# Seeding the accumulation bank with the running sum, one tile ahead, and moving five modulation tiles from the attention into the input projection

## The chip, the cores and the metric

The kernel runs on one core of one Trainium2 chip. The metric is the device time of one execution in microseconds (us); the kernel before takes 2125.85 us, the median of three runs (2124.03 to 2126.39). In what follows PE is TensorE (the matmuls), DVE is VectorE, ACT is ScalarE, POOL is GpSimd, and SP is the engine that issues most of the DMAs.

## The reference

It is one layer of a diffusion backbone: 512 latent tokens of width 2048, with 256 context tokens as a prefix that the attention reads. Cut to what matters:

```python
mod_l = (silu(c) @ w_ada + b_ada);  mod_c = (silu(c_ctx) @ w_ada + b_ada)
sh_a, sc_a, gt_a, sh_f, sc_f, gt_f = split(mod_l, 6)
h_l = modulate(rms_norm(x, g_mix_norm), sh_a, sc_a)        # h * (1 + scale) + shift
h_c = modulate(rms_norm(ctx, g_mix_norm), csh_a, csc_a)
qa, kva, kr, cb, cc, ch = split_projection(h_l @ w_in)     # 512, 256, 64, 3 x 1024 columns
k, v = mla_key_value(kva, kr, g_kv_a, w_kv_b, rope)        # the same for h_c
q = mla_query(qa, g_q_a, w_q_b, rope)
att = block_attention(q, [k_l, k_c], [v_l, v_c])           # 8 heads, softmax in f32
conv = cb * dwconv3(cc * ch, conv_w, conv_b)
x = x + gt_a * (rms_norm_per_group([att, conv]) @ w_out)
u = dwconv3(modulate(rms_norm(x), sh_f, sc_f) @ w_up);  a, g = split(u, 2)
x = x + gt_f * ((a * silu(g)) @ w_down)
return rms_norm(x, g_final)
```

The modulation vectors are products of one vector with the 2048 x 12288 matrix w_ada. The input projection has 3904 columns; transposed, these are 31 tiles of 128 columns by 512 tokens. The sum over the 2048 input features is 16 blocks of 128, called k-tiles below.

## The kernel before, in words

All large products keep float32 accuracy by splitting each operand into a high and a low part; every product is then three matmuls (mm3, lines 202 to 204). The split of a weight block is a cast on ACT for the high part (line 181) and a subtraction on DVE for the low part (line 182), from a raw buffer that a DMA has filled (line 150). There are two raw buffers for the weights of the projection.

The stages, by the trace: start until 24 us; input projection until about 396; preparation of queries, keys and values until about 447; attention in 32 steps until about 622; output projection until about 805; the gated MLP's up projection until about 1660; its down projection until the end.

The **input projection** goes through the 16 k-tiles in three chunks (ci = 0, 1, 2 with 2, 4 and 10 k-tiles), so that work can begin before all of the normalised input is there. Each chunk makes a partial sum for all 31 output tiles in PSUM. In chunks 1 and 2 the first six tiles (called pf) are computed together as rows; the other 25 (called pp) follow one after the other. In chunk 0 the partial sum of a tile is copied to a tile acc in SBUF by ACT. In chunks 1 and 2 the function evac adds the partial sum to acc on DVE (line 678):

```python
V.tensor_tensor(out=acc[m], in0=acc[m], in1=ps, op=ALU.add)
```

PSUM has eight banks. Four are handed out singly, four in two tiles of two banks each; two output tiles that share such a pair also share its waits, so that the first matmul into the second half waits for the read-out of the first half.

Beside this, **ctx_mods** (line 667) computes the context's 32 modulation columns with 64 products on DVE, called dots here. Each takes a half of a modulation tile (128 x 1024) that SP loads into one of four buffers; a new load must wait until a dot has freed its buffer. One or two dots are let loose per projection tile. Further modulation tiles, called **late**, are needed only after the attention. late_both lets one be loaded and an earlier one be multiplied; the loop of chunk 2 calls it at tiles i = 20 to 22 (two loads), and the attention's loop loads the rest at its steps n (late_load, line 1150 and those around it).

The order of the work on each engine is that of a scheduler that simulates the engines' timeline, except where keep(...) fixes program order. So a change in the program's text can also move instructions that it doesn't touch. The other two functions of the change are gn_sum (sums of squares per group, four one-column matmuls into one bank) and ctx_stats (the context's normalisation, spread over the partitions by a matmul into the bank rcb).

Of the kernel before, what the change touches and what calls it, by code (L numbers as in the profile page):

```python
# [11 lines left out]
F32R = mybir.dt.float32r  # L12
AF = mybir.ActivationFunctionType
ALU = mybir.AluOpType
# [17 lines left out]
G = 6  # L32
# [43 lines left out]
def block_kernel(ctx, tc, xt, ctxt, ctxn, c, c_ctx, w_ada, small, w_in, w_inc, w_q, w_kv, w_out,  # L76
# [313 lines left out]
    def gn_sum(t, o):  # L390
        sq = tmp([P, T], F32, f"gq{t}")
        A.activation(sq, o, AF.Square)
        yield
        ps = sml(f"gp{t}")
        for g in range(4):
            PE.matmul(ps[:, g:g + 1], sq[:, g * P:(g + 1) * P], ones[:, 0:1], start=True, stop=True)
        V.tensor_copy(out=gn[:, 4 * t:4 * t + 4], in_=ps[:, :4])
        yield

# [29 lines left out]
    with ExitStack() as pa:  # L429
# [197 lines left out]
        def ctx_stats():  # L627
            ss = tiny(4, "ss")
            for i in range(2):
                for q, r in enumerate(ada_tiles(p_sb, 4, ctxn[i], f"cn{i}")):  # L630
                    A.activation(r, r, AF.Square, accum_out=ss[:, 2 * i + q:2 * i + q + 1])
                    yield
            r = tiny(2, "rsc")
            V.tensor_tensor(out=r, in0=ss[:, 0:4:2], in1=ss[:, 1:4:2], op=ALU.add)
            rsqrt(r, r, D)
            yield
            pb = sml("rcb")
            spread(pb, r)
            A.copy(out=rc, in_=pb[:, :C])
            yield  # L640

        def ctx_prep(g):
# [27 lines left out]
        cm = ctx_mods()  # L670
        acc = {}

        def evac(ci, m, ps):
            if ci == 0:
                acc[m] = t2([P, T], F32, f"acc{m}")
                A.copy(out=acc[m], in_=ps)
                return
            V.tensor_tensor(out=acc[m], in0=acc[m], in1=ps, op=ALU.add)  # L678
            if ci < 2:
                return  # L680
            if m == 3:
                bg.appendleft(low_rank([acc[i] for i in range(4)], "g_q", T, "qa", qan))
            elif m == 5:
                bg.appendleft(low_rank([acc[i] for i in (4, 5)], "g_kv", T, "kl", kvl))
            elif m == 6:
                bg.appendleft(rope_key())
            elif m >= 9 and m % 3 == 0:
                q = bg if m < 27 else post
                q.append(conv((m - 9) // 3))
                q.append(gn_sum((m - 9) // 3, acc[m]))  # L690
                late_bg.append(gn_apply((m - 9) // 3, acc[m]))
# [137 lines left out]
        for ci, k0, n in ((1, K0[1], KCH[1]), (2, K0[2], KCH[2])):  # L829
# [21 lines left out]
            if ci == 1:  # L851
                ordered[0] = False
            per, step = max(1, 2048 // (n * P)), max(1, 4 // n)
            for i, m in enumerate(ORDER[G:]):
                if i % per == 0:
                    k = min(per, len(ORDER) - G - i) * n
                    raw = load(w_in[:, off:off + k * P], k * P, f"rw{ci}_{m}", G_ if ci == 1 else None)
# [1 line left out]
                if i % step == 0:  # L859
                    ws = blocks(raw, min(step, len(ORDER) - G - i) * n, f"w{ci}_{m}", i % per * n)  # L860
                w = ws[i % step * n:(i % step + 1) * n]
                ps = bank(f"pp{ci}_{m}")
                for kk in range(n):
                    mm3(ps, w[kk], hl[k0 + kk], kk == 0, kk == n - 1)
                evac(ci, m, ps)
                for f, j in todo.get((ci, i), []):
                    f(j)
                if ci == 2:
                    for q in range(2 if i % 4 == 0 else 1):
                        next(cm, None)  # L870
                    if 20 <= i <= 22:
                        late_both((lambda t: ada_tiles(p_sb, 4, w_ada[t], f"ae{t}")) if i < 22 else None)
                    if i >= 5 and i % 2 == 1 and (i - 5) // 2 < CTX_EARLY:
                        bg.append(ctx_prep((i - 5) // 2))
                    pump(2)
# [30 lines left out]
    with ExitStack() as pb:  # L906
# [215 lines left out]
        for n, st in enumerate(steps):  # L1122
# [23 lines left out]
                f(p_, i)  # L1146
            if at < 2 and n < 24:
                fetch(pr + 1, 2 + at)
            elif (at >= 2 or n == 24) and n <= 24:
                late_load(ada_raw)  # L1150
                if at == 6 and n < 16:
                    fetch(pr + 2, 0)
            if n == 8:
# [819 lines left out]
```

## Time and profile before

| | |
|---|---|
| median of three runs | 2125.85 us (2124.03 to 2126.39) |
| profiled execution | 2129.29 us |
| its span, first to last instruction | 2127.5 us |
| mean granted TensorE clock | 0.994 of full speed |
| PE busy | 2088.2 us (98%) |
| DVE busy | 1821.0 us (86%) |
| ACT busy | 1049.5 us (49%) |
| DMA | 514.78 MB, 242 GB/s on average |

A row of the profile names line, engine, operation, the tile written and the tiles read (buffer numbers left out), and the shapes. A bracket at its end gives the time that the engine stood idle before it and what released it. The granted clock is the share of full speed at which TensorE was allowed to run.

### The profile page before, as it was taken

Reading aid. Unit: us, or ns where it says so; the run is one execution under the profiler, and the core shown is the slowest. Engines: PE = TensorE matmul, PEld = TensorE weight load, DVE = VectorE, ACT = ScalarE, POOL = GpSimd, SP = SyncE. Lnnn points to the kernel's source line nnn. Section 1 sums busy time; section 2 is a strip of 40 time slices with the busy share of each in tenths; the row PEclk is TensorE's granted clock in tenths of the full one; section 3 lists DMA queues with packets and bytes.
Section 4 is the critical chain, followed back from the end, with each engine's and each line's share of the span. In section 5 each row is a group of like instructions: output and inputs, shape, how many; then the busy total and the mean of one; then the engine's idle time right before and its main releaser. Section 6 shows DMA issues by size and latency. Waiting matters only on the chain.

```text
span 2127.5 us, 35260 instructions
## 1 busy us (share of the span) xinstructions
PE 2088.2 (98%) x13303; PEld 1880.9 (88%) x13303; DVE 1821.0 (86%) x2952; ACT 1049.5 (49%) x1715; POOL 127.7 (6%) x161
## 2 busy tenths in 40 slices
PE   8999999999999999999999999999999999999997
PEld 6777778889888889999999999999999889999997
DVE  7898987878887888898999999999999659887887
ACT  6534233555552337555555655655555333333445
POOL 0000000000010000111000000000000000000000
PEclk9999999999999999999999999999999999999999
DMA  9799877435658975577888878888888989878684
GB/s 343 278 323 325 298 263 236 138 129 198 208 191 325 335 284 164 154 223 212 226 232 238 235 220 239 240 228 230 240 229 231 366 304 309 246 230 240 195 237 136
DMA packets 165885, 514.78 MB, mean 242 GB/s; under 512 B 18641, under 2 KB 22993, under 8 KB 155985
## 3 DMA queue, kind: packets, MB, share of 16 engines
q1 hardware_dynamic: 127024, 407.90, 56.7%
q0 software_dynamic: 19312, 70.40, 15.7%
q10 hardware_dynamic: 19378, 34.23, 4.2%
q8 instruction: 104, 1.70, 0.3%
q14 instruction: 67, 0.55, 0.1%
HBM read 465.26 MB, written 46.14 MB: 240 GB/s over the span
## 4 chain that ended last, share of the span: by engine, by line
PE 88%; DVE 5%; DMA 3%; issue 2%; ACT 2%; POOL 0%; DVEq 0%; SPq 0%; ACTq 0%; POOLq 0%
PE pp L202 3%; PE pp L204 3%; PE pp L203 3%; PE o L202 1%; PE o L204 1%; PE o L203 1%; PE d L202 1%; PE d L203 1%; PE d L204 1%; PE uf L202 1%; PE uf L203 1%; PE uf L204 1%; PE of L202 1%; PE of L204 1%; PE of L203 1%
## 5 line engine op out<-in xcount | busy, mean ns | idle before, releaser
L1445 POOL DMA_DIRECT2D u_s<-in_w_up x80 | 68.4, 855 | 682.5 <-DMA u_s<-in_w_up 402.9
L285 DVE SCALAR_TENSOR_TENSOR ada<-ada,sv 128x2048 f32<-128x2048 f32 x33 | 75.5, 2289 | 16.0 <-DMA ada<-in_w_ada 15.6
L181 ACT CAST w_0h<-rw 128x512 fp32r<-128x512 f32 x50 | 30.5, 620 | 99.2 <-DMA rw<-in_w_in 49.8
L667 DVE SCALAR_TENSOR_TENSOR ada<-ada,svc 128x1024 f32<-128x1024 f32 x64 | 76.1, 1217 | 1.9 <-DMA ada<-in_w_ada 1.9
L1566 DVE TENSOR_TENSOR u<-u,u_s 128x1024 f32<-128x1024 f32 x40 | 48.7, 1218 | 4.0 <-DMA u_s<-in_w_up 4.0
L281 DVE SCALAR_TENSOR_TENSOR ra<-ra,sv 128x1024 f32<-128x1024 f32 x42 | 49.8, 1216 | 0.0
L256 DVE SCALAR_TENSOR_TENSOR ada<-ada,sv 128x1024 f32<-128x1024 f32 x40 | 48.3, 1213 | 0.8 <-DMA ada<-in_w_ada 0.8
L1567 DVE TENSOR_TENSOR u<-u,u 128x1024 f32<-128x1024 f32 x40 | 48.6, 1216 | 0.0
L182 DVE TENSOR_TENSOR w_0l<-rw,w_0h 128x512 fp32r<-128x512 f32 x50 | 33.9, 682 | 15.4 <-ACT w_0h L181 15.2
L1071 POOL TENSOR_TENSOR gr<-gr,half 128x8 f32<-128x8 f32 x4 | 11.2, 2809 | 488.1 <-DVE gr L1070 458.1
L1365 DVE TENSOR_TENSOR tp<-a,tp 128x256 fp32r<-128x256 f32 x90 | 37.5, 416 | 2.9 <-ACT tp L1364 2.9
L1364 ACT CAST tp<-a 128x256 fp32r<-128x256 f32 x90 | 35.7, 403 | 6.6 <-DMA yl6h<-y_d 3.7
L1042 ACT CAST pth<-t 128x384 fp32r<-128x384 f32 x64 | 28.6, 486 | 18.0 <-PE t L1039 17.9
L1043 DVE TENSOR_TENSOR ptl<-t,pth 128x384 fp32r<-128x384 f32 x64 | 33.1, 548 | 3.9 <-ACT pth L1042 3.9
L1328 ACT ACTIVATE g<-g 128x512 f32<-128x512 f32 x43 | 27.2, 634 | 18.0 <-DVE g L1322 17.7
L678 DVE TENSOR_TENSOR acc<-acc,pp 128x512 f32<-128x512 f32 x50 | 33.8, 677 | 1.5 <-PE pp L204 1.5
L1021 DVE TENSOR_REDUCE mn<-s 128x1 f32<-128x768 f32 x32 | 30.3, 950 | 4.9 <-PE s L1010 4.9
L1320 ACT ACTIVATE g<-cg,sm 128x512 f32<-128x512 f32 x40 | 32.6, 815 | 0.0
L1320 ACT ACTIVATE a<-ca,sm 128x512 f32<-128x512 f32 x40 | 32.1, 802 | 0.0
L1024 ACT ACTIVATE p<-s,mn 128x768 f32<-128x768 f32 x32 | 29.3, 914 | 4.3 <-DVE mn L1021 4.1
L1321 DVE SCALAR_TENSOR_TENSOR g<-cg,sm,g 128x511 f32<-128x511 f32 x40 | 29.8, 745 | 0.0
L1321 DVE SCALAR_TENSOR_TENSOR a<-ca,sm,a 128x511 f32<-128x511 f32 x40 | 29.8, 745 | 0.0
(10435 smaller groups left out, 8966.4 us busy)
## 6 DMA issues: line engine op xcount, KB each, us to landing
ada<-in_w_ada SPq DMA_DIRECT2D x128, 512.0 KB, 5.9
u<-in_w_up SPq DMA_DIRECT2D x120, 512.0 KB, 9.2
w<-t_d SPq DMA_DIRECT2D x161, 256.0 KB, 5.3
u_s<-in_w_up SPq DMA_DIRECT2D x80, 512.0 KB, 4.0
u_s<-in_w_up POOLq DMA_DIRECT2D x80, 512.0 KB, 9.7
ada<-in_w_ada SPq DMA_DIRECT2D x33, 1024.0 KB, 6.2
t_d<-tp ACTq DMA_DIRECT2D x126, 256.0 KB, 6.0
v<-in_w_dnw SPq DMA_DIRECT2D x72, 384.0 KB, 5.7
```

The source lines that it names most:

```text
L202: PE.matmul(ps, w[0], x[0], start=first, stop=False, skip_group_check=on_top)
L203: PE.matmul(ps, w[0], x[1], start=False, stop=False, skip_group_check=on_top)
L204: PE.matmul(ps, w[1], x[0], start=False, stop=last, skip_group_check=on_top)
L256: ins = V.scalar_tensor_tensor(out=r, in0=r, scalar=1.0, in1=vec[:, i * 1024:(i + 1) * 1024], op0=ALU.mult, op1=ALU.mult, accum_out=col[:, ...
L281: keep(V.scalar_tensor_tensor(out=halves[i], in0=halves[i], scalar=1.0, in1=svs[i], op0=ALU.mult, op1=ALU.mult, accum_out=lc[:, t % 4:t % ...
L285: keep(V.scalar_tensor_tensor(out=r, in0=r, scalar=1.0, in1=sv, op0=ALU.mult, op1=ALU.mult, accum_out=mod[:, t:t + 1]))
L667: keep(V.scalar_tensor_tensor(out=raw[q], in0=raw[q], scalar=1.0, in1=svc[:, q * 1024:(q + 1) * 1024], op0=ALU.mult, op1=ALU.mult, accum_o ...
L1320: A.activation(u, src, AF.Identity, bias=s("fb", m), scale=s("fw", 86 + m))
L1321: V.scalar_tensor_tensor(out=u[:, 1:], in0=src[:, :T - 1], scalar=s("fw", m), in1=u[:, 1:], op0=ALU.mult, op1=ALU.add)
L1445: G_.dma_start(r[-1], src[more], accum_op=ALU.add)
L1566: V.tensor_tensor(out=a11, in0=a11, in1=s1, op=ALU.add)
L1567: V.tensor_tensor(out=a12, in0=a12, in1=a11, op=ALU.add)
```

## The change

Three things are different in the text.

1. In chunks 1 and 2, for the 25 pp tiles each: ACT copies acc into the PSUM bank of the **next** tile (seeded, line 864 of the changed kernel), before the current tile is multiplied. The matmuls then all add to what is in the bank (start=False), and ACT copies the finished sum back to acc (line 683). The addition on DVE stays for the six pf tiles of each chunk (line 685).
2. In gn_sum DVE writes zeros into the bank's four columns first, and its matmuls add to them; in ctx_stats a matmul with a zero operand is put behind the copy out of the bank rcb.
3. The loop of chunk 2 calls late_both at i = 17 to 24 in place of 20 to 22, with seven loads in place of two; the attention's loop has no late loads at steps 20 to 24 any more.

```diff
--- before.py
+++ after.py
@@ -392,8 +392,9 @@
         A.activation(sq, o, AF.Square)
         yield
         ps = sml(f"gp{t}")
+        V.tensor_scalar(ps[:, :4], ones[:, :4], scalar1=0.0, scalar2=None, op0=ALU.mult)
         for g in range(4):
-            PE.matmul(ps[:, g:g + 1], sq[:, g * P:(g + 1) * P], ones[:, 0:1], start=True, stop=True)
+            PE.matmul(ps[:, g:g + 1], sq[:, g * P:(g + 1) * P], ones[:, 0:1], start=False, stop=True, skip_group_check=True)
         V.tensor_copy(out=gn[:, 4 * t:4 * t + 4], in_=ps[:, :4])
         yield
 
@@ -637,6 +638,9 @@
             pb = sml("rcb")
             spread(pb, r)
             A.copy(out=rc, in_=pb[:, :C])
+            none = tmp([P, T], F32R, "none")[:, :P]
+            V.tensor_scalar(none, ones, scalar1=0.0, scalar2=None, op0=ALU.mult)
+            PE.matmul(pb, none, hl[K0[2]][0], start=False, stop=True, skip_group_check=True)
             yield
 
         def ctx_prep(g):
@@ -670,12 +674,15 @@
         cm = ctx_mods()
         acc = {}
 
-        def evac(ci, m, ps):
+        def evac(ci, m, ps, whole_sum=False):
             if ci == 0:
                 acc[m] = t2([P, T], F32, f"acc{m}")
                 A.copy(out=acc[m], in_=ps)
                 return
-            V.tensor_tensor(out=acc[m], in0=acc[m], in1=ps, op=ALU.add)
+            if whole_sum:
+                A.copy(out=acc[m], in_=ps)
+            else:
+                V.tensor_tensor(out=acc[m], in0=acc[m], in1=ps, op=ALU.add)
             if ci < 2:
                 return
             if m == 3:
@@ -851,7 +858,15 @@
             if ci == 1:
                 ordered[0] = False
             per, step = max(1, 2048 // (n * P)), max(1, 4 // n)
+
+            def seeded(m):
+                ps = bank(f"pp{ci}_{m}")
+                A.copy(out=ps, in_=acc[m])
+                return ps
+
+            nxt_ps = seeded(ORDER[G])
             for i, m in enumerate(ORDER[G:]):
+                ps, nxt_ps = nxt_ps, seeded(ORDER[G + i + 1]) if G + i + 1 < len(ORDER) else None
                 if i % per == 0:
                     k = min(per, len(ORDER) - G - i) * n
                     raw = load(w_in[:, off:off + k * P], k * P, f"rw{ci}_{m}", G_ if ci == 1 else None)
@@ -859,17 +874,16 @@
                 if i % step == 0:
                     ws = blocks(raw, min(step, len(ORDER) - G - i) * n, f"w{ci}_{m}", i % per * n)
                 w = ws[i % step * n:(i % step + 1) * n]
-                ps = bank(f"pp{ci}_{m}")
                 for kk in range(n):
-                    mm3(ps, w[kk], hl[k0 + kk], kk == 0, kk == n - 1)
-                evac(ci, m, ps)
+                    mm3(ps, w[kk], hl[k0 + kk], False, kk == n - 1, on_top=True)
+                evac(ci, m, ps, True)
                 for f, j in todo.get((ci, i), []):
                     f(j)
                 if ci == 2:
                     for q in range(2 if i % 4 == 0 else 1):
                         next(cm, None)
-                    if 20 <= i <= 22:
-                        late_both((lambda t: ada_tiles(p_sb, 4, w_ada[t], f"ae{t}")) if i < 22 else None)
+                    if 17 <= i <= 24:
+                        late_both((lambda t: ada_tiles(p_sb, 4, w_ada[t], f"ae{t}")) if i < 24 else None)
                     if i >= 5 and i % 2 == 1 and (i - 5) // 2 < CTX_EARLY:
                         bg.append(ctx_prep((i - 5) // 2))
                     pump(2)
@@ -1146,8 +1160,9 @@
                 f(p_, i)
             if at < 2 and n < 24:
                 fetch(pr + 1, 2 + at)
-            elif (at >= 2 or n == 24) and n <= 24:
-                late_load(ada_raw)
+            elif at >= 2 and n < 24:
+                if n < 20:
+                    late_load(ada_raw)
                 if at == 6 and n < 16:
                     fetch(pr + 2, 0)
             if n == 8:
```

How this moves instructions at three places:

The first place is the start of chunk 2's pp tiles, tiles 13 and 14, which share a pair of banks. On DVE before, with the pf additions of chunk 2 (pf20 to pf24), dots of ctx_mods (ada180, ada181) and the addition of tile 13 (acc13):

```order
L678 TENSOR_TENSOR acc8_403<-acc8_403,pf21_1555 128x512
L678 TENSOR_TENSOR acc9_405<-acc9_405,pf22_1556 128x512
L182 TENSOR_TENSOR w2_14_0l_1975<-rw2_14_1972,w2_14_0h_1974 128x512
L307 SCALAR_TENSOR_TENSOR scc0_2553<-modc_91,sm_82 128x2
L678 TENSOR_TENSOR acc10_407<-acc10_407,pf23_1557 128x512
L667 SCALAR_TENSOR_TENSOR ada181_1712,lcc_281<-ada181_1712,svc_99 128x1024
L678 TENSOR_TENSOR acc11_431<-acc11_431,pf24_1558 128x512
L678 TENSOR_TENSOR acc12_433<-acc12_433,pf24_1558 128x512
L604 TENSOR_TENSOR acc7_401<-acc7_401,acc8_403 128x512
L678 TENSOR_TENSOR acc13_435<-acc13_435,pp2_13_1924 128x512
L182 TENSOR_TENSOR w2_15_0l_2029<-rw2_15_2026,w2_15_0h_2028 128x512
```

On ACT in the changed kernel, at the same place, with the seeds of tiles 15 to 18, the casts of the weights of tiles 14 and 15, and the copy of tile 13's sum:

```order
L864 COPY pp2_15_2002<-acc15_468 128x512
L181 CAST w2_14_4h_2010<-rw2_14_2004 128x512
L864 COPY pp2_16_2058<-acc16_470 128x512
L608 ACTIVATE acc8_403<-acc7_401,sm_82 128x512
L640 COPY rc_280<-rcb_1783 128x256
L181 CAST w2_14_8h_2014<-rw2_14_2004 128x256
L864 COPY pp2_17_2119<-acc17_500 128x512
L864 COPY pp2_17_2119<-acc18_502 128x512
L181 CAST w2_15_0h_2062<-rw2_15_2060 128x512
L181 CAST w2_15_4h_2066<-rw2_15_2060 128x512
L683 COPY acc13_435<-pp2_13_1938 128x512
```

The read-out of tile 13 has gone from DVE, where it stood behind the pf additions, to ACT, where it stands behind two casts of tile 15's weights and four seeds.

The second place is SP's queue around the weights of tiles 20 to 22 of chunk 2 (rw2_20 to rw2_22), with halves of modulation tiles (ada) between them. Before:

```order
L150 DMA rw2_20_2317<-in_w_in 128x1280
L150 DMA ada231_2133<-in_w_ada 128x1024
L150 DMA ada70_2187<-in_w_ada 128x1024
L150 DMA ada71_2189<-in_w_ada 128x1024
L150 DMA ada240_2193<-in_w_ada 128x1024
L150 DMA ada241_2195<-in_w_ada 128x1024
L150 DMA ada80_2252<-in_w_ada 128x1024
L150 DMA ada81_2254<-in_w_ada 128x1024
L150 DMA rw2_21_2376<-in_w_in 128x1280
L150 DMA ada250_2308<-in_w_ada 128x1024
L150 DMA ada251_2310<-in_w_ada 128x1024
L150 DMA rw2_22_2438<-in_w_in 128x1280
```

Now:

```order
L150 DMA rw2_20_2358<-in_w_in 128x1280
L150 DMA ada231_2168<-in_w_ada 128x1024
L150 DMA ada70_2222<-in_w_ada 128x1024
L150 DMA ada71_2224<-in_w_ada 128x1024
L150 DMA ada240_2228<-in_w_ada 128x1024
L150 DMA rw2_21_2418<-in_w_in 128x1280
L150 DMA ada241_2230<-in_w_ada 128x1024
L150 DMA ada80_2290<-in_w_ada 128x1024
L150 DMA ada81_2292<-in_w_ada 128x1024
L150 DMA rw2_22_2481<-in_w_in 128x1280
L150 DMA ada250_2347<-in_w_ada 128x1024
L150 DMA ada251_2349<-in_w_ada 128x1024
```

The seven halves between the weights of tiles 20 and 21 have become four.

The third place is DVE near the end of the attention: the softmax maxima of successive steps (mn), the dots of the last late tiles (ra53, ra54), the splits of the output projection's first weights (ofw0) and the scaling of two output tiles (o4, o5). Before:

```order
L281 SCALAR_TENSOR_TENSOR ra54_5702,lc_94<-ra54_5702,sv_93 128x1024
L403 SCALAR_TENSOR_TENSOR acc21_559<-acc21_559,sm_82,gb4_5735 128x512
L1021 TENSOR_REDUCE mn70_5807<-s70_5761 128x1
...
L281 SCALAR_TENSOR_TENSOR ra53_5629,lc_94<-ra53_5629,sv_93 128x1024
...
L1021 TENSOR_REDUCE mn71_5842<-s71_5823 128x1
L182 TENSOR_TENSOR ofw0_0l_6042<-ofr0_5924,ofw0_0h_6041 128x512
L182 TENSOR_TENSOR ofw0_4l_6046<-ofr0_5924,ofw0_4h_6045 128x512
...
L182 TENSOR_TENSOR ofw0_8l_6050<-ofr0_5924,ofw0_8h_6049 128x512
L1081 SCALAR_TENSOR_TENSOR o4_5261<-o4_5261,sm_82,gb4_5793 128x512
L1081 SCALAR_TENSOR_TENSOR o5_5537<-o5_5537,sm_82,gb5_5799 128x512
```

Now:

```order
L281 SCALAR_TENSOR_TENSOR ra53_5416,mod_90<-ra53_5416,sv_93 128x1024
L281 SCALAR_TENSOR_TENSOR ra53_5416,lc_94<-ra53_5416,sv_93 128x1024
...
L281 SCALAR_TENSOR_TENSOR ra54_5470,mod_90<-ra54_5470,sv_93 128x1024
L281 SCALAR_TENSOR_TENSOR ra54_5470,lc_94<-ra54_5470,sv_93 128x1024
L182 TENSOR_TENSOR ofw0_0l_6113<-ofr0_5995,ofw0_0h_6112 128x512
L182 TENSOR_TENSOR ofw0_4l_6117<-ofr0_5995,ofw0_4h_6116 128x512
...
L1035 TENSOR_REDUCE mn53_5594<-s53_5564 128x1
L182 TENSOR_TENSOR ofw0_8l_6121<-ofr0_5995,ofw0_8h_6120 128x512
...
L1035 TENSOR_REDUCE mn60_5664<-s60_5612 128x1
```

Relative to the softmax steps, the last dots and the splits of ofw0 come five to seven steps earlier.

## Prediction

> **What bounds the kernel now.** I read the page's busy times and chain first, then the windows by stage, and after that the timelines of the stages that the change touches. The page says that the program is a row of matmuls:
>
> ```profile
> PE 2088.2 (98%) x13303; PEld 1880.9 (88%) x13303; DVE 1821.0 (86%) x2952; ACT 1049.5 (49%) x1715; POOL 127.7 (6%) x161
> ...
> PE 88%; DVE 5%; DMA 3%; issue 2%; ACT 2%; POOL 0%; DVEq 0%; SPq 0%; ACTq 0%; POOLq 0%
> ```
>
> TensorE is busy for 2088.2 of 2127.5 us. Nothing in the change takes matmuls away, so all that it can win is time in which TensorE stands still, plus time in which it runs at a lowered clock. The windows (columns: length, then busy time of PE, PEld, DVE, ACT, POOL, granted clock, DMA share, GB/s) tell in which stage that is:
>
> ```profile
> 88.00:158.00 70.00, 69.53 (x300) 56.07 (x299) 70.00 (x135) 26.65 (x40) 2.65 (x5) 1.00 0.87 307
> 158.00:316.00 158.00, 147.51 (x630) 118.58 (x629) 137.96 (x272) 52.93 (x96) 0.00 (x0) 0.96 0.86 297
> 316.00:360.00 44.00, 44.00 (x190) 35.40 (x189) 34.75 (x67) 13.19 (x24) 0.00 (x0) 1.00 0.83 280
> 344.00:412.00 68.00, 67.37 (x304) 54.12 (x302) 51.87 (x99) 29.32 (x58) 0.00 (x0) 1.00 0.47 157
> ```
>
> The second chunk of the projection (88 to 158) keeps TensorE full, although VectorE is full as well. From 316 on TensorE is full again, at 44.00/190 = 0.232 us a matmul. Only 158 to 316, the third chunk's first half, loses 10.5 us of busy time and has a clock of 0.96. The timeline of TensorE there names the stalls (idle time and releaser in brackets):
>
> ```profile
> 214.26 0.79 PE L202 MATMUL pp<-h6h,w_0h 128*128 128x512 f32 x1 [4.25 <-DVE acc L678]
> 247.33 0.51 PE L202 MATMUL pp<-h6h,w_0h 128*128 128x512 f32 x1 [1.41 <-ACT w_0h L181]
> 248.35 0.50 PE L204 MATMUL pp<-h6h,w_0l 128*128 128x512 f32 x1 [0.28 <-DVE w_0l L182]
> 280.28 0.50 PE L202 MATMUL pp<-h6h,w_0h 128*128 128x512 f32 x1 [2.48 <-ACT w_0h L181]
> 281.95 0.80 PE L204 MATMUL pp<-h6h,w_0l 128*128 128x512 f32 x1 [0.85 <-DVE w_0l L182]
> ```
>
> They are 4.25 + 1.69 + 3.33 = 9.27 us. After the first and the last the clock drops, in windows laid on its steps:
>
> ```profile
> 212.49:219.32 6.83, 5.06 (x12) 4.00 (x13) 6.83 (x12) 0.81 (x1) 0.00 (x0) 0.50 0.71 243
> 246.63:253.46 6.83, 5.85 (x24) 4.46 (x25) 6.83 (x14) 1.77 (x3) 0.00 (x0) 1.00 0.93 306
> 280.76:287.59 6.83, 5.98 (x15) 4.46 (x14) 6.83 (x12) 2.69 (x7) 0.00 (x0) 0.50 0.87 267
> ```
>
> At clock 0.50 work of 5.06 us would have taken half, so the first drop costs 2.53 us and the other 5.98/2 = 2.99 us; behind the 1.41 us wait the clock stays at 1.00. The stage's recoverable time is 9.27 + 2.53 + 2.99 = 14.8 us.
>
> [...]
>
> **Why these stalls are there.** The 4.25 us stall waits for the addition of acc13 on VectorE (L678). What VectorE does ahead of it:
>
> ```profile
> 206.30 0.69 DVE L678 TENSOR_TENSOR acc<-acc,pf 128x512 f32<-128x512 f32 x1 [0.98 <-PE pf L204]
> ...
> 206.97 1.22 DVE L667 SCALAR_TENSOR_TENSOR ada<-ada,svc 128x1024 f32<-128x1024 f32 x1
> ...
> 208.12 1.28 DVE L678 TENSOR_TENSOR acc<-acc,pf 128x512 f32<-128x512 f32 x2
> ...
> 210.59 1.22 DVE L667 SCALAR_TENSOR_TENSOR ada<-ada,svc 128x1024 f32<-128x1024 f32 x1
> ...
> 211.73 1.28 DVE L678 TENSOR_TENSOR acc<-acc,pf 128x512 f32<-128x512 f32 x2
> 212.93 0.68 DVE L604 TENSOR_TENSOR acc<-acc,acc 128x512 f32<-128x512 f32 x1
> 213.53 0.68 DVE L678 TENSOR_TENSOR acc<-acc,pp 128x512 f32<-128x512 f32 x1
> ```
>
> The sum is ready well before 213.53, but six pf additions, two dots and a conv product stand in front of it in VectorE's order. Tile 14 lies in the same two-bank PSUM tile as tile 13, and its first matmul may not start until tile 13 is read out.
>
> The stalls at 247 and 280 are late weights. The queue of SP, and ScalarE's next cast:
>
> ```profile
> 247.72 12.37 SPq L150 DMA_DIRECT2D ada<-in_w_ada  x7
> 260.76 0.33 SPq L150 DMA_DIRECT2D rw<-in_w_in  x1
> ...
> 267.35 0.62 ACT L181 CAST w_0h<-rw 128x512 fp32r<-128x512 f32 x1 [8.51 <-DMA rw<-in_w_in]
> ```
>
> SP issues seven modulation halves in a row and needs 12.37 us for them, because each waits for a dot on VectorE to give back one of four buffers; the weights of tile 21 stand behind them and land so late that ScalarE idles 8.51 us. VectorE being behind is therefore the cause of both kinds of stall, and the change takes work from VectorE.
>
> **The change, part by part.**
>
> ```profile
> L181 ACT CAST w_0h<-rw 128x512 fp32r<-128x512 f32 x50 | 30.5, 620 | 99.2 <-DMA rw<-in_w_in 49.8 <-PE pp L203 39.5 <-PE pf L203 4.9
> L667 DVE SCALAR_TENSOR_TENSOR ada<-ada,svc 128x1024 f32<-128x1024 f32 x64 | 76.1, 1217 | 1.9 <-DMA ada<-in_w_ada 1.9
> L678 DVE TENSOR_TENSOR acc<-acc,pp 128x512 f32<-128x512 f32 x50 | 33.8, 677 | 1.5 <-PE pp L204 1.5
> L281 DVE SCALAR_TENSOR_TENSOR ra<-ra,sv 128x1024 f32<-128x1024 f32 x42 | 49.8, 1216 | 0.0
> ...
> L736 ACT COPY acc<-pp x23: 573/604/662, 45.0 to 72.4; 128x512 f32<-128x512 f32 x23
> ```
>
> *Seeding.* The 50 pp additions leave VectorE: 33.8 us, half in each chunk. ScalarE gets 100 copies. The one from PSUM has its row (L736, 0.60 us); the one into PSUM has none, and I bound it by the shortest L736 copy, 0.57, and the like-sized cast from SBUF, 0.62; with 0.60 the sum is 60 us on ScalarE. In 88 to 316 ScalarE is busy 26.65 + 52.93 = 79.6 of 228 us, and three quarters of the copies fall there, so it stays under 60%: covered. [...] A seed does not stand directly before its tile in ScalarE's new order but two to six tiles ahead, so TensorE should not wait for one.
>
> What I gain from it: VectorE reaches the third chunk with 16.9 us less done, and the modulation dots move up into that room; acc13 is read by a copy on ScalarE that has no pf additions ahead of it. So the 4.25 us stall and its 2.53 us go. In SP's new order three or four halves, not seven, stand between two weight loads, so 1.69 + 3.33 + 2.99 = 8.0 us can go too. The second part has a limit. The DMA share over 158 to 316 is 0.86, that is 136 us of transfers; the busiest long stretch is this:
>
> ```profile
> 158.00:205.00 47.00, 46.29 (x200) 37.26 (x199) 38.36 (x76) 20.51 (x34) 0.00 (x0) 1.00 0.92 326
> ```
>
> At 0.92 those 136 us need 148, so 10.3 us can be won if the same transfers stay in the stage, and 14.9 by the same division over 88 to 316 (0.86 and 0.87) if some move ahead. Between 10.3 and 14.8 I take 12.5.
>
> What it costs: the second tile of a two-bank pair waits for the copy of the first. In chunk three I count 2, 3, 6, 6 and 6 matmuls of a later tile between them at the five shortest places (w_14, w_18, w_22, w_1, w_30), 0.46 to 1.39 us of cover. If ScalarE is free the copy costs 0.14 us once and nothing else. If two casts of the next tile stand ahead of it and have just been released, it ends 2 x 0.62 + 0.60 = 1.84 us later, less the cover: 1.38 + 1.15 + 3 x 0.45 = 3.9 us. I take 1.5, a little under the middle: before the change the same late weights would have stopped TensorE in their own right. In chunk two the cover is 23 to 27 matmuls: nothing.
>
> *The zero writes and the zero matmul.* One 128x512 matmul is 0.23 us on the path. Eight four-column writes and one 128x128 product on VectorE lie in stages where TensorE is full; uncovered, they would be under 0.2 us each by the smallest VectorE rows in the stall's timeline, 1.6 us at most.
>
> *The moved tiles.* Five tiles are ten dots, 10 x 1.216 = 12.2 us, and ten loads of 512 KB. They leave the attention for 344 to 412, where VectorE is busy 51.87 of 68 us, has some eight additions less (5.4 us), and ends at 59 of 68; DMA is at 0.47 there. SP gets them ahead of the last weight loads, but the dots they wait for stand, on VectorE, ahead of the splits that those weight loads wait for anyway: nothing, and 1 us if one split slips. At the attention's end they bring this back:
>
> ```profile
> 597.36 1.21 DVE L281 SCALAR_TENSOR_TENSOR ra<-ra,sv 128x1024 f32<-128x1024 f32 x1
> 598.50 1.22 DVE L281 SCALAR_TENSOR_TENSOR ra<-ra,sv 128x1024 f32<-128x1024 f32 x1
> ...
> 601.25 1.21 DVE L281 SCALAR_TENSOR_TENSOR ra<-ra,sv 128x1024 f32<-128x1024 f32 x1
> ```
>
> ```profile
> 608.07 0.65 PE L324 MATMUL gb<-io,gn 128*128 128x128 f32 x4 [1.35 <-DVE o L1081]
> 609.22 0.50 PE L1006 MATMUL s<-kl31h,q31h 128*128 128x512 f32 x1 [0.50 <-ACT p L1024]
> ```
>
> The last dots and the first splits of the output weights stand ahead of the o product there; in the new order both come several softmax steps earlier. I book both waits, 1.85 us.
>
> *The sum.* 12.5 + 1.85 - 1.5 - 0.2 = 12.65 us less. The profiled execution took 2129.3 us with what lies around its span, so 2116.6 for it; the median of the runs, 2125.85, is 3.4 us lower, which gives **2113 us**.
>
> **Rivals.** *Only the read-out stall goes.* The raw weights still have two buffers, and a load cannot start before the split of two tiles ago, so rw may land as late as now. For it: the stall at 280 comes after the burst, behind a lone late load. Against it: splits are what VectorE now reaches earlier. Then 4.25 + 2.53 + 1.85 - 1.7 = 6.9 us: 2119.
>
> *Nothing moves.* The stage at 0.86 may already be as fast as its transfers, mixed from two streams, can go; TensorE then waits for rw what it waited for acc13. Against it: 0.92 over 47 us. What is left is 1.85 - 1.7: 2126. The change would then not do what it says, since ScalarE's casts, and with them its read-outs, would be as late as VectorE's additions.
>
> *Slower: ScalarE's queue becomes the wait.* The copy that frees a pair stands behind casts of the next tile, and these wait for its weights:
>
> ```profile
> ACT w_0h L181 <- DMA rw<-in_w_in: 36.8, 8, 8.5
> ```
>
> That is 36.8/8 = 4.6 us a wait (ScalarE, 88 to 316). Where the landing comes 4.6 us after the pair's first tile has ended, TensorE stops for 4.6 + 0.62 + 0.60 - 1.4 of cover = 4.4 us and loses some 2.8 by the clock: 7.2 us a place, at five places. Three such places are 21.6 us against the 16.6 that go (14.8 + 1.85): 2125.85 + 5 = 2131. It decides from three on. Against it: before shows only two places with late weights, and none of over 2.48 us.
>
> **How the numbers follow.** Forecast 0.60, with a range of its own of 2108 (all 16.6 us and a little more behind it) to 2118; only the read-out stall 0.18; nothing 0.12; slower 0.10. The range for 8 in 10 reaches from 2105, where further small VectorE waits of the attention go too, to 2127, past the case of no change. A measurement of this kernel tells about 0.2% from no change, here 4.3 us: under 2121.6 lie nearly all of the forecast and most of the first rival, 0.58 + 0.14 + 0.02 = 0.74; within, 0.16; above 2130.1, 0.10 by the last rival and strays.
>
> **What would show it.** Right: no idle row over 2 us on TensorE in 158 to 316, clock 1.00 there, SP's longest run of modulation halves under 6 us, the third chunk's last tile ending some 12 us earlier, the attention's end 2 us shorter. If clocks of 0.50 remain behind w_0h waits, the first rival holds; if the idle rows before second tiles of a pair name ACT acc, the last. A DMA share of 0.86 with idle spread anew would speak for no change. I would be wrong altogether if TensorE waited for seeds, or if VectorE were not ahead at 316.

## The result

The changed kernel takes 2109.66 us (median of six runs, 2109.33 to 2115.66), the kernel before, run beside it, 2124.49 us. The ratio is 0.9937, with a 95% interval of 0.9924 to 0.9950: 13.4 us less at that ratio, where 12.65 us were forecast. 2109.66 lies inside the forecast's own range, 3.3 us under its middle; 1.4 us of these are the kernel before, which the forecast took at 2125.85 us.

The profiled executions differ by more, 19.8 us of span (2127.5 and 2107.7). A part of that is not the change's, as the last section shows.

### The profile page after: what moved, and what is told of

Same layout as the page of the kernel before. It is cut to its first block, busy times and chain, and to the rows that moved or that the text cites. A ratio compares the mean times of both kernels' runs of the same rounds, so it can differ in the third digit from the quotient of the medians.

```text
span 2107.7 us, 35339 instructions
## 1 busy us (share of the span) xinstructions
PE 2080.4 (99%) x13304; PEld 1875.2 (89%) x13304; DVE 1792.8 (85%) x2911; ACT 1100.6 (52%) x1815; POOL 126.8 (6%) x161
## 4 chain that ended last, share of the span: by engine, by line
PE 87%; DVE 5%; DMA 4%; issue 2%; ACT 2%; POOL 0%; DVEq 0%; POOLq 0%; ACTq 0%; SPq 0%
PE pp L202 3%; PE pp L204 3%; PE pp L203 3%; DMA rw<-in_w_in 2%; PE o L202 1%; PE o L204 1%; PE o L203 1%; PE d L202 1%; PE d L203 1%; PE d L204 1%; PE uf L202 1%; PE uf L203 1%; PE uf L204 1%; PE of L202 1%; PE of L204 1%
## 5 line engine op out<-in xcount | busy, mean ns | idle before, releaser
L1085 POOL TENSOR_TENSOR gr<-gr,half 128x8 f32<-128x8 f32 x4 | 10.3, 2580 | 474.9 <-DVE gr L1084 427.8
L281 DVE SCALAR_TENSOR_TENSOR ra<-ra,sv 128x1024 f32<-128x1024 f32 x32 | 38.0, 1216 | 0.0
L683 ACT COPY acc<-pp 128x512 f32<-128x512 f32 x49 | 28.3, 580 | 5.3 <-PE pp L204 5.3
```

The costliest lines, as they stand in the source:

```text
L281: keep(V.scalar_tensor_tensor(out=halves[i], in0=halves[i], scalar=1.0, in1=svs[i], op0=ALU.mult, op1=ALU.mult, accum_out=lc[:, t % 4:t % ...
```

## The profile after

From the page of the changed kernel, the busy times and, of the groups, the copies back (count, then busy us and mean ns); and then, from the answer on line 864, the seeds (min/median/max ns):

```profile
PE 2080.4 (99%) x13304; PEld 1875.2 (89%) x13304; DVE 1792.8 (85%) x2911; ACT 1100.6 (52%) x1815; POOL 126.8 (6%) x161
...
L683 ACT COPY acc<-pp 128x512 f32<-128x512 f32 x49 | 28.3, 580 | 5.3 <-PE pp L204 5.3
```

```profile
L864 ACT COPY pp<-acc x49: 577/591/595, 73.8 to 362.4; 128x512 f32<-128x512 f32 x49
```

VectorE has lost 28 us and ScalarE has gained 51, by two copies a tile of 0.591 us (median of the seeds) and 0.580 us (mean of the copies back). By these rows the 100 copies come to 58.6 us, and the 50 additions that left VectorE to 33.8 us. The totals move by less, since the records of neighbouring instructions overlap by some 0.1 us, as in the rows of ScalarE below. The price of the seed, for which no row stood before, was taken as 0.60. TensorE is busy for 7.8 us less with one matmul more: 5.5 us were the two stretches at half clock. The rest, 2.3 us, was not taken apart; the matmul rate of the last section has a part in it.

The windows of the projection (length, then PE, PEld, DVE, ACT, POOL busy, clock, DMA share, GB/s):

```profile
88.00:158.00 70.00, 69.86 (x300) 55.90 (x299) 63.09 (x123) 51.14 (x88) 2.65 (x5) 1.00 0.90 336
158.00:316.00 158.00, 157.27 (x695) 126.94 (x694) 140.25 (x281) 77.00 (x142) 0.00 (x0) 1.00 0.92 327
```

From 158 to 316 us TensorE is now busy for 157.27 us at full clock and runs 695 matmuls where it ran 630. The DMA share has gone from 0.86 to 0.92, as much as the best long stretch had shown before, and the second chunk has taken up more transfers too, 0.90 for 0.87. The two stalls that are left in this stage, from TensorE's timeline:

```profile
210.40 0.50 PE L202 MATMUL pp<-h6h,w_0h 128*128 128x512 f32 x1 [0.27 <-ACT acc L683]
...
240.90 0.50 PE L202 MATMUL pp<-h6h,w_0h 128*128 128x512 f32 x1 [0.27 <-ACT acc L683]
```

They are the waits for a pair's read-out by ScalarE that the forecast priced at 1.5 us; they cost 0.54 us. ScalarE at the first of them:

```profile
207.84 0.62 ACT L181 CAST w_0h<-rw 128x512 fp32r<-128x512 f32 x1 [0.56 <-PE pp L203]
209.24 0.63 ACT L181 CAST w_4h<-rw 128x512 fp32r<-128x512 f32 x1 [0.78 <-PE pp L203]
209.78 0.57 ACT L683 COPY acc<-pp 128x512 f32<-128x512 f32 x1
```

The casts ahead of the copy are released by TensorE, not by a late load, and the copy runs the moment they are through. The queue of SP has its longest run of modulation halves at 270.76:

```profile
247.21 0.38 SPq L150 DMA_DIRECT2D rw<-in_w_in  x1
249.65 4.48 SPq L150 DMA_DIRECT2D ada<-in_w_ada  x3
254.23 0.38 SPq L150 DMA_DIRECT2D rw<-in_w_in  x1
...
270.76 7.11 SPq L150 DMA_DIRECT2D ada<-in_w_ada  x4
```

That is 7.11 us for four, the longest run from 200 to 292 us, where seven took 12.37. Where the time goes by stage is read from the first matmul of the query preparation (pq) and of the attention (s). From the answers on those two tiles, before and then after (min/median/max ns, then first and last start in us):

```profile
L202 PE MATMUL pq<-qa0h,wq00h x1: 475/475/475, 394.8 to 394.8; 128*128 128x512 f32 x1
...
L1006 PE MATMUL s<-kl00h,q00h x3: 388/499/500, 437.0 to 449.5; 128*128 128x512 f32 x3
```

```profile
L202 PEld LDWEIGHTS pq<-qa0h,wq00h x1: 192/192/192, 380.4 to 380.4; 128*128 128x128 f32 x1
...
L1020 PE MATMUL s<-kl00h,q00h x4: 389/491/504, 422.9 to 437.9; 128*128 128x512 f32 x4
```

The projection hands over 14.4 us earlier (394.8 to 380.4), the preparation loses 0.3 of it (14.1 at the first step of the attention), and by the output projection's first matmul the lead is 14.8 us (624.4 and 609.6). So nearly everything comes from the projection.

## The experiments

Twelve runs follow, the last two rows of the table being repeats. The table has the lead of each kernel over the kernel before at the two places just named, in us from the traces (a negative lead is a delay), and the ratio of the times:

| kernel | seeded | moved tiles | lead at pq | lead at s | ratio (95%) |
|---|---|---|---|---|---|
| the change | chunks 1, 2 | five | 14.4 | 14.1 | 0.9937 (0.9924 to 0.9950) |
| seeding only | 1, 2 | none | 15.5 | 16.5 | 0.9944 (0.9931 to 0.9958) |
| moved tiles only | none | five | 1.1 | -8.3 | 1.0042 (1.0029 to 1.0055) |
| chunk 1 | 1 | five | 11.0 | 1.9 | 0.9994 (0.9985 to 1.0002) |
| chunk 2 | 2 | five | 13.9 | 13.6 | 0.9945 (0.9932 to 0.9957) |
| chunk 1, no move | 1 | none | 11.8 | 11.6 | 0.9955 (0.9941 to 0.9969) |
| seed at its own tile | 1, 2 | five | 14.1 | 13.6 | 0.9937 (0.9923 to 0.9951) |
| half dots | none | none | 10.5 | 10.5 | 0.9951 (0.9936 to 0.9966) |
| copy back on VectorE | 1, 2 | none | 7.2 | 5.2 | 0.9983 (0.9974 to 0.9993) |
| chunk 1, half late dots | 1 | five | 9.5 | 9.1 | 0.9946 (0.9933 to 0.9959) |
| two tiles moved | 1, 2 | two | 14.5 | 15.4 | 0.9933 (0.9921 to 0.9945) |
| the change, again | 1, 2 | five | 13.3 | 11.6 | 0.9934 (0.9923 to 0.9946) |
| seeding only, again | 1, 2 | none | 15.5 | 16.5 | 0.9929 (0.9917 to 0.9941) |

### The two halves of the change

The seeding alone, from the changed kernel (the attention's loads go back as well):

```diff
-                    if 17 <= i <= 24:
-                        late_both((...) if i < 24 else None)
+                    if 20 <= i <= 22:
+                        late_both((...) if i < 22 else None)
...
-            elif at >= 2 and n < 24:
-                if n < 20:
-                    late_load(ada_raw)
+            elif (at >= 2 or n == 24) and n <= 24:
+                late_load(ada_raw)
```

> The whole change without its move of five modulation tiles. Theory (VectorE being behind is what stalls TensorE in the third chunk, and the seeding relieves it): nearly all of the gain stays, 12 to 14 us under the kernel before, all of it before the attention begins; the attention's end keeps its waits of 1.35 and 0.50 us. Rival (the moved tiles carry a large part): 8 us under the kernel before or less.

Its ratio is 0.9944, 12 us less. The attention's end keeps its waits. From the waits of TensorE in this kernel (total us, times, longest):

```profile
PE gb L324 <- DVE o L1095: 1.2, 1, 1.2
...
PE s L1020 <- ACT p L1038: 1.1, 2, 0.6
```

The theory holds: the seeding carries the gain. The moved tiles alone are the reverse of that diff, put on the kernel before:

> The kernel before with the move of the five modulation tiles alone. Theory: 0 to 2 us faster, the two waits at the attention's end gone, the stalls of 4.25, 1.69 and 3.33 us and both clock drops in the projection unchanged. Rival (the moved tiles carry a large part): 5 us faster or more. Second rival (they hurt the projection's last tiles when VectorE has not been relieved): 2 us slower or more, with new waits between 360 and 400 us.

They make the kernel 0.42% slower, 9 us. The second rival of that text was right, and so was its place, though the larger wait comes a little later than it said. ScalarE's timeline and, behind it, TensorE's:

```profile
414.08 1.09 ACT L653 ACTIVATE cr<-cr,modc,scc 128x256 f32<-128x256 f32 x2 [1.12 <-DVE cr L652]
...
416.16 0.58 ACT L920 COPY xq<-pq 128x512 f32<-128x512 f32 x1
```

```profile
416.79 1.22 PE L408 MATMUL qr<-xq,kc 128*128 128x512 f32 x1 [4.55 <-ACT xq L920]
```

In the preparation for the attention ScalarE copies the query's rotary part (xq) only after the context tokens' rows, and these wait for VectorE (L652), which has spent 12 us on the ten dots that came here. TensorE idles for 4.55 us. The row shows 1.12 us of waiting for VectorE; that the dots cause the whole wait is tested below, on a kernel that seeds chunk 1. An earlier wait, for weights of the query preparation at 394 us, takes 1.2 us. The mean granted clock of this execution is 0.993, that of the kernel before 0.994. The projection's stalls are still there: 4.23 us at tile 14, and 4.1 us for late weights in place of 5.0. So booking the moved tiles at nothing holds only where something else in the same change makes room on VectorE.

### Which chunk's seeding counts

For one chunk alone, whole is true only there, and elsewhere the tile starts its own sum and VectorE adds it (the second and third chunk of the expectations are chunks 1 and 2):

```diff
-            nxt_ps = seeded(ORDER[G])
+            whole = ci == 1          # 2 in the other kernel
+            nxt_ps = seeded(ORDER[G]) if whole else None
...
-                    mm3(ps, w[kk], hl[k0 + kk], False, kk == n - 1, on_top=True)
-                evac(ci, m, ps, True)
+                    mm3(ps, w[kk], hl[k0 + kk], kk == 0 and not whole, kk == n - 1, on_top=whole)
+                evac(ci, m, ps, whole)
```

> The change with the seeding in the second chunk alone (25 additions off VectorE before the third chunk begins); in the third chunk VectorE adds again. Theory of the lag: VectorE arrives 17 us less behind, so the late-weight stalls and their clock drop (6.3 us of 9.3 in all with the drop of 3) mostly go and the 4.25 us stall shrinks to under 2.5 us, below the point of the clock drop: 8 to 12 us faster. Rival (what counts is that the read-out of the third chunk's tiles no longer stands in VectorE's order): 0 to 3 us faster, the 4.25 us stall still there.

> The change with the seeding in the third chunk alone. Theory of the lag: the 4.25 us stall goes, because ScalarE reads out tile 13, with its clock drop (6.8 us); the stalls for late weights at 247 and 280 us become smaller only step by step, as 25 additions leave VectorE during the chunk: 7 to 10 us faster. Rival (read-out's place is all): 13 us faster, like the whole change. Second rival (with VectorE still behind, ScalarE's copies wait for casts and these for weights): 0 to 4 us faster, with idle rows before second tiles of a pair that name the acc copy.

Seeding chunk 2 alone gives nearly all of it, 0.9945 with a lead of 13.9 us. Ahead of tile 14 TensorE waits 0.80 us for the seed of tile 15, and not for the read-out of tile 13:

```profile
211.29 0.51 PE L202 MATMUL pp<-h6h,w_0h 128*128 128x512 f32 x1 [0.80 <-ACT pp L864]
```

The ratio is worth 11.7 us, more than the 7 to 10 us of the lag theory and near the first rival's number: the late weights at 247 and 280 go at once, not step by step. For the late weights place and lag are not told apart by it, since the 25 read-outs and their time leave VectorE together. For the read-out of tile 13 they are: VectorE begins its last pf additions there at 212.72 us, no earlier than before (211.73), and the stall is gone all the same. Seeding chunk 1 alone makes no difference that can be told, 0.9994. But its trace has a lead of 11.0 us at pq, which it loses by the attention's first step; the wait for xq is there again, of 4.9 us. So two readings were left: the move does it, or the seeding of chunk 1 only shifts VectorE's backlog. The same kernel without the moved tiles:

> Seeding in the second chunk alone, without the moved tiles. With the moved tiles this seeding was 11 us ahead of the kernel before at the last projection tile and had lost 9 of it by the first attention step. Theory (the loss is the moved tiles' dots on a VectorE that still has the third chunk's additions): 9 to 12 us faster than before. Rival (the loss is the second chunk's seeding itself, which only shifts VectorE's backlog to a later place): 0 to 4 us faster.

0.9955, 9.6 us less, and a lead of 11.6 us at the attention. The loss is the moved tiles'. Of the stalls of chunk 2 only one is left, 2.24 us for a split; nothing waits for the read-out of tile 13. VectorE's timeline, with its last pf additions and that read-out:

```profile
204.38 1.28 DVE L685 TENSOR_TENSOR acc<-acc,pf 128x512 f32<-128x512 f32 x2
...
212.54 0.68 DVE L685 TENSOR_TENSOR acc<-acc,pp 128x512 f32<-128x512 f32 x1
```

The pf additions are through at 205.66 us, ahead of the end of tile 13's sum at 209.2, but the read-out is still 3.3 us late. It holds nobody up because the scheduler has changed TensorE's order too: 14 matmuls of tile 15 come between tile 13 and tile 14, where the kernel before has two, and the pf tiles are finished before tile 13 begins. So this kernel is not a test of VectorE's time alone.

Both chunks' seeding together wins 15.5 us at pq, one or the other 11 to 14: the gains don't add, because either relief already ends most of the same stalls.

Dots or loads? Chunk 1 seeded, five tiles moved, and the dots of the projection's seven late tiles over half their columns (so those modulation sums cover half the features), with every load as it was:

```diff
+            w = 512 if t < 39 else 1024
-            keep(V.scalar_tensor_tensor(out=halves[i], in0=halves[i], ..., in1=svs[i], ...
+            keep(V.scalar_tensor_tensor(out=halves[i][:, :w], in0=halves[i][:, :w], ..., in1=svs[i][:, :w], ...
```

> Seeding in the second chunk alone with the five moved tiles, where the dots of the seven late tiles of the projection run over 512 of 1024 columns (so these modulation sums cover half the features); the loads are as before. Theory (the moved dots' VectorE time, some 14 x 0.6 us here, is what delays the preparation for the attention): the 4.9 us wait for xq goes or falls under 2 us, 6 to 10 us faster than before. Rival (the loads ahead of the last weights in SP's queue are the cost): the wait stays above 4 us, 0 to 3 us faster than before.

The waits for xq with whole dots, and then with half dots:

```profile
PE qr L409 <- ACT xq L936: 5.7, 2, 4.9
```

```profile
PE qr L410 <- ACT xq L937: 0.7, 1, 0.7
```

The ratio goes from 0.9994 to 0.9946 with the same loads. The wait of 4.9 us before the attention is gone; the 0.7 us are another one, inside the attention, that was 0.78 us with whole dots. So that wait comes from VectorE's time on the dots (16.7 us for the 14 of them, now 9.1). What the loads themselves cost is not told apart: the lead at pq, 9.5 us, is 2.3 us below that without the moved tiles.

### VectorE's time, or the place of the read-out

The kernel before, with the 64 dots of the context's modulation over half their columns (those sums cover half the features), so that VectorE has 33 us less to do (76.1 to 42.8 us by the dots' rows; the text below says 39) and each read-out is VectorE's as before:

```diff
-                    keep(V.scalar_tensor_tensor(out=raw[q], in0=raw[q], ..., in1=svc[:, q * 1024:(q + 1) * 1024], ...
+                    keep(V.scalar_tensor_tensor(out=raw[q][:, :512], in0=raw[q][:, :512], ..., in1=svc[:, q * 1024:q * 1024 + 512], ...
```

> The kernel before, with each of the 64 dots for the context's modulation taken over 512 of its 1024 columns (so these modulation sums cover half the features): some 0.6 us less on VectorE for each, 39 us in all, with every load, addition and read-out as before. Theory of the lag (only VectorE's time in the projection counts): the stalls of the third chunk go or shrink below the point of the clock drop, 10 to 15 us faster, though every read-out still is VectorE's. Rival (the read-out must leave VectorE's queue): the 4.25 us stall stays within 1 us of its size, 0 to 5 us faster.

Both texts are half right. TensorE's stall at tile 14 and SP's longest run of halves after 240 us in this kernel:

```profile
212.75 0.80 PE L202 MATMUL pp<-h6h,w_0h 128*128 128x512 f32 x1 [3.09 <-DVE acc L678]
```

```profile
263.75 6.65 SPq L150 DMA_DIRECT2D ada<-in_w_ada  x3
```

The late weights are cured by VectorE's time alone: the burst of seven is gone, and none of the 5.0 us of waits between 240 and 316 us is left. The wait for tile 13's read-out is not: 3.09 of 4.25 us stay, since the pf additions still stand ahead of it. VectorE's first pf additions there, and the read-out:

```profile
205.93 1.28 DVE L678 TENSOR_TENSOR acc<-acc,pf 128x512 f32<-128x512 f32 x2 [0.57 <-PE pf L204]
...
212.02 0.68 DVE L678 TENSOR_TENSOR acc<-acc,pp 128x512 f32<-128x512 f32 x1
```

VectorE is not behind at this place: it idles 0.57 us until TensorE has finished a pf tile. Then it works through six pf additions, two dots, a split and a conv product before it comes to tile 13. The gain is 10.4 us.

The opposite case keeps VectorE's load and takes the addition away: ScalarE seeds, VectorE copies back (without the moved tiles).

```diff
             if whole_sum:
-                A.copy(out=acc[m], in_=ps)
+                V.tensor_copy(out=acc[m], in_=ps)
```

> Seeding as in the change and no moved tiles, but VectorE copies the finished sum back, so that VectorE has 50 copies in place of 50 additions and ScalarE 50 copies more than before. Theory of the lag: VectorE is as loaded as before, so the stalls come back: within 3 us of the kernel before. Rival (adding inside PSUM itself is what helps): 10 us faster or more.

```profile
L683 DVE COPY acc<-pp x49: 672/680/692, 95.2 to 401.2; 128x512 f32<-128x512 f32 x49
```

```profile
214.54 0.80 PE L202 MATMUL pp<-h6h,w_0h 128*128 128x512 f32 x1 [3.43 <-DVE acc L683]
```

A copy costs VectorE 0.680 us, the addition 0.677, so the load is the same, and the stall at tile 14 is back with 3.43 us. The kernel is still 0.17% faster than before (interval 0.07% to 0.26%), 3.6 us, where the theory said within 3. The late-weight stall at 247 us is there with 1.14 us, the one at 280 us is missing. In SP's queue the weights of tile 21 go out at 258.65, not 260.76, behind six halves and not seven. That this alone ends the second late-weight stall was not tested.

### One tile ahead

```diff
-            nxt_ps = seeded(ORDER[G])
...
-                ps, nxt_ps = nxt_ps, seeded(ORDER[G + i + 1]) if G + i + 1 < len(ORDER) else None
+                ps = seeded(m)          # just ahead of the tile's matmuls
```

> The whole change, but each bank is seeded when its own tile comes, not one tile ahead. If one tile ahead matters, the seed of a pair's second half has to wait for the copy out of the first half, and TensorE waits for both, some 1.2 us less the cover at each of the pairs of the third chunk: 3 to 8 us slower than the whole change, with idle rows that name the seed copy (ACT pp). Rival (the scheduler puts the copies where it likes anyway): within 1.5 us of the whole change.

```profile
PE pp L202 <- ACT pp L864: 1.4, 3, 0.9
```

Three waits for a seed, 1.4 us together, and the same ratio as the change, 0.9937. The rival was right. In ScalarE's order the seeds of tiles 15, 16 and 17 have kept their places, and only those of a pair's second half (tiles 14 and 18) come later, right behind the copy that reads out the first half. So little hangs on where the text asks for the seed.

### The moved tiles once the seeding is there

The changed kernel and the seeding alone were run once more, side by side on one chip, and with them a kernel that moves two tiles in place of five:

```diff
-                    if 17 <= i <= 24:
-                        late_both((...) if i < 24 else None)
+                    if 19 <= i <= 23:
+                        late_both((...) if i < 23 else None)
...
-                if n < 20:
+                if n < 22:
```

> The changed kernel itself, beside the next kernel on the same chip, for the size of the moved tiles' effect when the seeding is there. From the traces: the tiles cost 2.4 us between the last projection tile and the attention's first step and give back 0.7 at the attention's end, so it should be 1 to 2 us slower than the seeding without the moved tiles. Rival (the earlier medians, 2109.7 against 2111.5, are right): 2 us faster.

> The seeding in both chunks without the moved tiles, again, beside the changed kernel on the same chip. Theory from the traces: 1 to 2 us faster than the changed kernel. Rival from the earlier medians: 2 us slower than it.

> The seeding as in the change, but two late tiles are moved from the attention (its steps 22 to 24) in place of five. If each moved tile's two dots cost a fifth of the 2.4 us before the attention and the attention's end gains as soon as its last dots come a few steps earlier: 1 us faster than both the change and the seeding without moved tiles. If the gain at the attention's end needs all five: 0 to 1 us slower than the seeding alone.

Medians of 2111.87, 2110.34 and 2110.94 us, ratios of 0.9934, 0.9929 and 0.9933: no difference that these runs can tell. In the traces the change lags the seeding alone by 1.1 us at pq and 2.4 us at the first attention step in one pair, 2.2 and 4.9 us in the other, and gets back 0.6 to 0.7 us by the output projection. Neither the five tiles nor two of them make the kernel better than the seeding does, and no version here beats the changed kernel by more than the runs can tell.

## Why the prediction was right

*Where the time was.* The stalls named (4.25, 1.69, 3.33 us) and the two clock drops are gone, all 14.8 us of them, against a lead of 14.4 us at pq. The step on the DMA limit was sized too low: 12.5 us were taken between 10.3 and 14.8, but the share did rise to 0.92 and the second chunk took over transfers, which was the upper bound's reason. The 14.9 us of that working is a slip: with 0.87 for the second chunk the division gives 14.1, so the middle would have been 12.2.

*Why they were there.* That VectorE's being behind is the cause of both kinds of stall was true for one kind. Half dots cure the late weights and leave 3.09 us of the read-out stall. The forecast's own row at 206.30 us speaks against it there: VectorE has just been idle for 0.98 us, waiting for a pf tile. The stall comes from what stands between that moment and the read-out in VectorE's order. It ends when the read-out leaves that queue (chunk 2's seeding, with the pf additions as late as before), or when TensorE has other work in the meantime: with chunk 1's seeding alone the read-out is still 3.3 us late, but more of tile 15 is multiplied ahead of tile 14, and what TensorE waits for, 2.2 us, is a split.

*What it costs.* 0.54 us for the pairs' waits, not 1.5. ScalarE stayed at 77.00 of 158 us. The last rival, ScalarE's queue as the new wait, did not come: ScalarE still waits for weights, 28.2 us in nine waits of up to 4.6 us from 88 to 302 us, but ahead of TensorE's need. In the second execution of the changed kernel one such wait reached TensorE, with 1.23 us.

*The moved tiles.* This step failed. They were booked as free where they go and as 1.85 us at the attention's end. Of the end's waits the one for o is gone and the one for p is 0.25 us in place of 0.50, but a wait of 0.70 us for xq inside the attention is new, and the attention as a whole is only 0.7 us shorter. Up to its first step the changed kernel lags the seeding alone by 2.4 and 4.9 us in the two pairs of traces, so the tiles are worth nothing that can be measured. The check was VectorE's busy time over 344 to 412, estimated at 59 of 68 us and now 55.19. A busy share does not show such a delay: TensorE waits 0.97 and 2.38 us (in the two executions) for ScalarE's copy of xq in the preparation. Where chunk 2 is not seeded the same step costs 8 to 9 us.

*The signs to look for.* Clock 1.00 and no idle row over 2 us came. SP's longest run is 7.11 us, not under 6. The projection ends 14.4 us earlier, not 12, and the attention is shorter by 0.7 us, not 2.

*What was luck.* The mechanism for the late weights and for the read-out's new place held, but the closeness of the total is in part luck: the stalls were booked too low and their cost too high, and the moved tiles, booked as a gain of 1.85 us, made up for a part of that by bringing none.

## What to carry to other kernels

A sum that spans several passes can be kept in PSUM by copying the running sum into the bank and letting the matmuls add to it. Here that took the addition of 0.677 us off VectorE, for two copies on ScalarE of 0.591 and 0.580 us. The zero writes of gn_sum and the zero matmul belong to every seeded kernel here; what would happen without them no run shows. Ask of a stall both how late the engine is and what stands ahead of the awaited instruction on it: in this kernel the first went when VectorE had less to do, the second only with another queue or another order. A row in which the engine itself is idle shortly before says that it is not late at that moment. And a step that is free because another part of the same change has just made room should be priced without that part too.

## What the runs showed of the hardware

**Half clock after one stall and not after its like.** The two kernels that seed chunk 1 alone have the same stall of 2.2 us at 212 us, a wait for a low part (w_0l), without and with the moved tiles. The rows around it without the moved tiles (length, then PE, PEld, DVE, ACT, POOL busy, granted clock, DMA share, GB/s):

```profile
208.81:212.22 3.41, 1.17 (x5) 0.65 (x4) 3.41 (x9) 1.43 (x2) 0.00 (x0) 1.00 0.67 218
212.22:215.63 3.41, 3.41 (x9) 2.64 (x9) 3.41 (x6) 0.00 (x0) 0.00 (x0) 0.50 0.89 308
```

And with them:

```profile
207.70:211.12 3.42, 2.16 (x10) 1.40 (x8) 3.42 (x6) 1.95 (x3) 0.00 (x0) 1.00 0.59 175
211.12:214.53 3.41, 2.44 (x11) 2.00 (x12) 3.41 (x8) 0.01 (x1) 0.00 (x0) 1.00 0.88 289
214.53:217.94 3.41, 3.41 (x16) 2.77 (x15) 3.41 (x6) 0.81 (x2) 0.00 (x0) 1.00 0.90 306
```

In the first, 2.24 us of 3.41 are idle, and the next 3.41 us run at a granted clock of 0.50, with 9 matmuls where a full row of the second kernel has 16. In the second, 2.23 us of 6.83 are idle, and the clock is 1.00 in all three rows. The idle time of one row does not tell the cases apart either. In the kernel that copies back on VectorE:

```profile
386.84:390.25 3.41, 2.42 (x15) 1.85 (x14) 3.41 (x10) 1.70 (x4) 0.00 (x0) 1.00 0.25 77
390.25:393.67 3.42, 3.42 (x10) 2.67 (x9) 3.25 (x8) 1.78 (x3) 0.00 (x0) 0.50 0.67 192
```

And in the kernel before, in the attention:

```profile
605.02:608.44 3.42, 2.07 (x19) 1.84 (x18) 3.42 (x6) 2.13 (x6) 0.00 (x0) 1.00 0.71 276
608.44:611.85 3.41, 2.91 (x20) 2.45 (x19) 3.00 (x6) 0.98 (x3) 0.00 (x0) 1.00 0.59 225
```

0.99 us of idle time in a row is followed by a row at half clock in the one, 1.35 us is not in the other; what decides it, no run here shows. So the forecast's two cases, 1.41 us without a drop and 2.48 us with one, don't make a threshold, though some of the expectations speak of a point of the clock drop. The two stalls of 2.2 us differ in price by 1.7 us or more, as an estimate from the row at 0.50 (half of its 3.41 us).

**A matmul rate with two values.** In the down projection, 100 us in the middle of it, in the profile before and in the one after:

```profile
1800.00:1900.00 100.00, 100.00 (x836) 100.00 (x835) 86.32 (x125) 38.49 (x46) 5.26 (x7) 1.00 0.80 245
```

```profile
1800.00:1900.00 100.00, 100.00 (x845) 100.00 (x845) 86.19 (x125) 39.30 (x47) 5.96 (x7) 1.00 0.79 242
```

TensorE is full at clock 1.00 in both, with 836 and 845 matmuls: 120.0 ns from start to start in one, 118.7 in the other (a window's count also takes in matmuls that reach over its edges). Whether the rate goes with the change these two rows don't tell. Over the some 320 us of 128x256 matmuls in this stage it is some 3.5 us, and it explains that much of the 19.8 us between the two profiles; another 1.2 us is a wait for a split near the end of the down projection (v20q4l) that the profile after does not have. What sets the rate stays open. The profiled execution of the kernel before, 2129.29 us, lies 4.80 us above the median of its runs (2124.49), that of the changed kernel, 2109.51 us, 0.15 us under its own; so 4.95 us of the 19.8 are not in the difference of the medians.
